# A streaming encoder step on one core: projection fills ranked by stage, merge weights in the fills' buffers, smaller pieces in the delta rule

## The chip, the cores and the metric

The kernel runs on one core of a Trainium2 chip. The metric is the device time of one execution in microseconds (us); it is the median of several executions. All arithmetic is float32: each big product is made of three matmuls of rounded parts (high by high, low by high, high by low), so one column block of weights always comes as a high tile (`whi`) and a low tile (`wlo`) that ScalarE and VectorE split from the raw block (`raw`).

## What is computed

The reference, cut to the parts that the change touches. 1152 tokens (a prompt of 1024 and 8 samples of 16) go through one layer of width 1024.

```python
h = rmsnorm(x)
z = h @ W_in                      # fq fk fv ff | gqkv ga gb gg | gate_a gate_b
yA = fox(fq, fk, fv, logf) @ w_proj_fox       # 8 heads x 64, 256 cached keys per sample
q, k, v = silu(short_conv(gqkv))              # width 4; its last 3 inputs are an output
o = gated_delta_rule(q, k, v, g, beta)        # chunks of 64 tokens, one after the other
yB = (rmsnorm(o) * silu(gg)) @ w_proj_gdn
x += rmsnorm((sigmoid(gate_a) * yA + sigmoid(gate_b) * yB) @ w_out)
x += rmsnorm(relu(rmsnorm(x) @ w_up) ** 2 @ w_down)
```

## The kernel before

The tokens are kept transposed, in high and low parts (`hhi`, `hlo`), as 9 tiles of 128 and 3 chunks of 384. The stages, in us of the profiled execution: the norm and the first transposes up to 50; the delta rule (GDN) for its four head pairs, 50 to 700; attention (FoX) for its four head pairs, 700 to 982; the merge, 982 to 1110; the output projection to 1227; the MLP to the end.

Each engine runs its instructions in a fixed order. That order is made ahead of time by a list scheduler that goes by priorities: `tc.high_priority(n)` ranks what is under it n places ahead of where it is written, and a negative n ranks it behind.

**Fills.** 32 column blocks of W_in are not needed where they are computed: gg, fq, fk and fv of the four head pairs (16 blocks, the list `todo`), then the merge's gates (16 more). Each is three chunks of 24 matmuls of 384 columns into the PSUM bank `mf`. ScalarE copies a chunk into the buffer `gst` and sends it to DRAM (`gg_d`, `fr_d`, `gate_d`), from where it is read back. `fill()` writes all of them (but the first) ahead of the delta rule with the priority -LOW, LOW = 100000: behind everything else, so that they run where TensorE has nothing else ready. Their weights lie in the pool `wp` (tag "f": FRB = 2 raw buffers, FHB = 3 high and low ones); the delta rule's own columns of W_in (bank `mm`) take theirs from `ww` (tag "w": RAWB = 1 raw buffer, 2 high and low ones).

**Delta rule.** For a head pair p, `gdn_in` multiplies the q, k and v columns; `gdn_conv` applies the convolution and the silu and sends out the last three inputs of the prompt and of each sample: a transpose on TensorE and a copy out of PSUM for each of 12 blocks, `lr` being the tile that GpSimd fills and that both go through. `gdn_systems` scales q, k and v and makes the decays and the systems of all 24 chunk units; `gdn_inverse` inverts them; `gdn_b` runs the recurrence over the chunks, for each of which TensorE waits in turn for `R` (L620), for `vn` (L623) and for `S` (L629) of VectorE. The copy `xs<-S` (L618) stands between them on VectorE. The products of `gdn_systems` over all 1152 tokens are single instructions on VectorE or GpSimd: on VectorE qs (L489), kb (L492), the decay's mask (L497) and half of qa (L508); on GpSimd vs (L477), ks (L486), the decay (L496) and the other half of qa (L508).

**Attention.** `fox_past` first reorders the columns of the cached log forget values by head pair with two GpSimd copies (L935), then transposes them on TensorE (L937).

**Merge.** `load` brings 24 blocks of attention and delta rule outputs back from DRAM (`orw`) and splits them into `ohi` and `olo`. For each of 8 column blocks j, `weights` loads and splits w_proj_fox and w_proj_gdn into buffers of the pool `op` (3 raw, 4 high and low), and six groups of 12 matmuls follow. A product with the sigmoid of a gate (`ga`) goes to `mt`; the sum of two is split into `hhi` and `hlo`, over the columns that the fills have been reading till then. `wo_part` loads the output projection's weights (`wor`).

## Time and profile before

| | |
|---|---|
| median of 3 executions | 1946.63 us (1942.45 to 1948.23) |
| the profiled execution | 1936.76 us, its span 1935.1 us |
| mean granted TensorE clock | 0.989 |
| TensorE busy | 1863.4 us, 96% of the span, 11036 matmuls |
| VectorE, ScalarE, GpSimd busy | 66%, 52%, 12% |

The profile is of one execution. A stretch of it is read by its busy times; a wait of an engine is named by the instruction that released it. TensorE runs nearly all the time, so a microsecond counts where TensorE stands still or works at a lower clock. A matmul's row is longer than its share of the time, since the next one starts before it ends.

### The profile page before, as it was taken

The numbers are of one execution on the slowest core, as the hardware profiler recorded it, in microseconds if no ns is written. First come the engines' busy times: TensorE is split into PE (matmuls) and PEld (weight loads), VectorE is DVE, ScalarE is ACT, GpSimd is POOL, SyncE is SP. The second block draws the span as 40 slices with busy tenths as digits, with TensorE's granted clock in tenths as the row PEclk, the third lists the DMA queues.
The fourth block names the chain that finished last, engine by engine and source line by source line (L and its number), as shares of the span: only waits on it lengthen the run. The fifth ranks groups of instructions, "written<-read, shape, count | busy, mean of one in ns | idle before, by whom it ended". The sixth has DMA issues, their size and how long they took to land.

```text
span 1935.1 us, 31957 instructions
## 1 busy us (share of the span) xinstructions
PE 1863.4 (96%) x11036; PEld 1689.2 (87%) x11036; DVE 1274.6 (66%) x3013; ACT 1001.1 (52%) x2382; POOL 232.6 (12%) x356
## 2 busy tenths in 40 slices
PE   7989999899999989999999999999999999999998
PEld 6979989899889987787899988999999998888886
DVE  6356587667774466766654455887677764559697
ACT  6344375464564665655554353555554554445553
POOL 2131251422512120000002200000000000000000
PEclk9999999999999999999999999999999999999999
DMA  6142413423335264433364462234444468845474
GB/s 197 45 102 69 114 47 91 106 63 106 84 87 166 76 186 141 132 109 110 89 196 138 139 206 89 65 115 131 139 137 132 145 186 296 289 149 183 149 261 137
DMA packets 293069, 261.34 MB, mean 135 GB/s; under 512 B 68876, under 2 KB 247368, under 8 KB 292908
## 3 DMA queue, kind: packets, MB, share of 16 engines
q1 hardware_dynamic: 252864, 225.10, 39.3%
q10 hardware_dynamic: 40044, 34.21, 5.4%
q8 instruction: 87, 1.43, 0.3%
q14 instruction: 74, 0.61, 0.1%
HBM read 186.48 MB, written 72.75 MB: 134 GB/s over the span
## 4 chain that ended last, share of the span: by engine, by line
PE 80%; DVE 6%; DMA 5%; ACT 4%; issue 3%; POOL 2%; SPq 0%; DVEq 0%; ACTq 0%; POOLq 0%
PE mm L158 47%; PE mf L158 14%; PE pc L1019 2%; PE pa L158 1%; PE pc L158 1%; PE pd L158 1%; PE pe L158 1%; PE pb L158 1%; DVE xs L618 1%; PE mm L1048 1%; DMA gate_d<-gst 1%; DMA out_dram<-kst 1%; PE pb L1010 1%; PE pc L633 1%; PE pa L461 1%
## 5 line engine op out<-in xcount | busy, mean ns | idle before, releaser
L158 PE MATMUL mf<-hhi,wlo 128*128 128x384 f32 x744 | 262.1, 353 | 2.4 <-DVE wlo L335 2.4
L158 PE MATMUL mf<-hhi,whi 128*128 128x384 f32 x744 | 261.1, 351 | 1.8 <-ACT gst L219 1.8
L158 PE MATMUL mf<-hlo,whi 128*128 128x384 f32 x744 | 261.9, 352 | 0.0
L158 PE MATMUL mm<-th,wh 128*128 128x320 f32 (+1 forms) x896 | 177.2, 293 | 0.0
L158 PE MATMUL mm<-bh,al 128*128 128x512 f32 x436 | 169.7, 389 | 0.0
L158 PE MATMUL mm<-bl,ah 128*128 128x512 f32 x436 | 169.6, 389 | 0.0
L158 PE MATMUL mm<-bh,ah 128*128 128x512 f32 x436 | 169.6, 389 | 0.0
L334 ACT CAST ah<-ar 128x512 fp32r<-128x512 f32 x107 | 66.4, 622 | 152.9 <-PE mm L158 101.1
L158 PEld LDWEIGHTS mf<-hhi,wlo 128*128 128x128 f32 x744 | 141.7, 190 | 3.6 <-DVE wlo L335 3.3
L158 PEld LDWEIGHTS mf<-hhi,whi 128*128 128x128 f32 x744 | 141.8, 191 | 2.4 <-ACT gst L219 2.1
L158 PEld LDWEIGHTS mm<-th,wh 128*128 128x128 f32 x896 | 142.9, 187 | 0.0
L158 PEld LDWEIGHTS mf<-hlo,whi 128*128 128x128 f32 x744 | 141.9, 191 | 0.7
L158 PE MATMUL mm<-th,wl 128*128 128x256 f32 x448 | 131.4, 293 | 0.0
L1381 DVE TENSOR_TENSOR s<-mm,s 128x256 f32<-128x256 f32 (+1 forms) x196 | 84.2, 453 | 66.2 <-PE mm L158 53.2
L335 DVE TENSOR_TENSOR al<-ar,ah 128x512 fp32r<-128x512 f32 x107 | 73.5, 688 | 74.6 <-ACT ah L334 73.9
L335 DVE TENSOR_TENSOR wlo<-raw,whi 128x512 fp32r<-128x512 f32 x110 | 76.8, 703 | 67.3 <-ACT whi L334 63.2
L158 PE MATMUL mm<-hhi,whi 128*128 128x384 f32 x288 | 103.9, 361 | 2.4 <-ACT whi L334 2.1
L158 PE MATMUL mm<-hhi,wlo 128*128 128x384 f32 x288 | 101.0, 351 | 2.1 <-DVE wlo L335 2.1
L158 PE MATMUL mm<-hlo,whi 128*128 128x384 f32 x288 | 102.5, 356 | 0.0
L334 ACT CAST whi<-raw 128x512 fp32r<-128x512 f32 x110 | 67.6, 620 | 62.2 <-PE mf L158 26.2
L158 PE MATMUL mm<-mhi,wl 128*128 128x256 f32 (+1 forms) x336 | 98.6, 293 | 0.0
L158 PE MATMUL mm<-mlo,wh 128*128 128x256 f32 (+1 forms) x336 | 98.6, 293 | 0.0
(543 smaller groups left out, 4949.3 us busy)
## 6 DMA issues: line engine op xcount, KB each, us to landing
ar<-ua_d SPq DMA_DIRECT2D x124, 256.0 KB
raw<-in_w_in_dram SPq DMA_DIRECT2D x86, 256.0 KB
br<-in_w_down_dram SPq DMA_DIRECT2D x78, 256.0 KB
wr<-in_w_up_dram SPq DMA_DIRECT2D x56, 256.0 KB
ua_d<-s SPq DMA_DIRECT2D x112, 128.0 KB
ua_d<-s ACTq DMA_DIRECT2D x84, 128.0 KB
gate_d<-gst ACTq DMA_DIRECT2D x48, 192.0 KB
ga<-gate_d SPq DMA_DIRECT2D x48, 192.0 KB
```

Of the source, the lines that this page charges most:

```text
L158: T.matmul(out, a, b, start=first and i == 0, stop=last and i == n - 1)
L334: A.copy(h, raw)
L335: V.tensor_tensor(l, raw, f(h), ALU.subtract)
L461: T.matmul(nps[:, t:t + NTT + 1:NTT], sq[:, t * P:(t + 1) * P], ones2, start=True, stop=True)
L618: (A.copy if h else V.tensor_copy)(xs[0:64, h], st_[64 * h:64 * h + 64])
L633: T.matmul(po[:, i * P:(i + 1) * P], xs[k0:].rearrange("p h c -> p (h c)"), qa[k0:, u].rearrange("p h c -> p (h c)"), start=True, stop=True)
L1010: T.transpose(tp[:, jj * 256 + qi * P:jj * 256 + qi * P + P], pr[qi][:, j * P:(j + 1) * P], ident)
L1019: T.matmul(acc[:, q0:256], v2[:, 2 * jp + jj, P * hh:P * hh + P], q[:, jj * 256 + q0:jj * 256 + 256], start=jp == 0 and jj == 0 and k == 0 ...
L1048: T.matmul(a[32 * b:32 * b + 32, P:384], qbd[:, b].rearrange("p h t -> p (h t)"), kt, start=True, stop=True)
L1381: V.tensor_tensor(r, o, x, ALU.add)
```

## The change

Seven edits: (1) `fill()` ranks the 15 first blocks 1400 places behind where they are written (RANKA) and the 16 gate blocks 3300 (RANKB), in place of 100000 for all; (2) more buffers: raw tiles of "w" 1 to 2, its high and low tiles 2 to 3, those of "f" 3 to 4, `gst` 1 to 2; (3) the last inputs of the convolution are kept in one tile `lrs` and go out once, at p == 2, by a function of their own, with 4 transposes a bank; (4) the convolution's prompt columns are done in two halves, after the samples; (5) the products qs, kb, the mask's sum and qa of the delta rule are done in halves; (6) the reordering of past's columns moves from the start of attention to p == 2 of the delta rule, into a tile of its own; (7) the merge's first weights (j == 0) take the fills' buffers, the others 2 raw and 3 high and low buffers in place of 3 and 4. Lines of the changed file lie up to 20 further down.

```diff
-RAWB = 1
+RAWB = 2
-FHB = 3
+FHB = 4
+RANKA = 1400
+RANKB = 3300
...
-    WBUFS = {"w": (RAWB, 2), "f": (FRB, FHB)}
+    WBUFS = {"w": (RAWB, 3), "f": (FRB, FHB)}
...
-               lambda c, acc: spill_out(wps_[tag], tag + "g", 1, w0, dst, c, acc), tag=(acc, nb), prio=prio)
+               lambda c, acc: spill_out(wps_[tag], tag + "g", 2, w0, dst, c, acc), tag=(acc, nb), prio=prio)
     def fill():
-        with tc.high_priority(-LOW):
-            for w0, dst in todo[NE:]:
-                spill(w0, dst, "f", "mf", 20, MFB)
+        for rank, part in ((RANKA, todo[NE:4 * NP_]), (RANKB, todo[4 * NP_:])):
+            with tc.high_priority(-rank):
+                for w0, dst in part:
+                    spill(w0, dst, "f", "mf", 20, MFB)
...
     def gdn_conv(gp, p, i, x):
-        lr = big(gp, "lr", 1, [P, 2, P])
-        G.memset(lr[:, 0], 0.0)
-        G.tensor_copy(lr[:, 0, 0:3], x[:, NPR:NPR + 3])
-        G.tensor_copy(lr[:, 0, 3:27].rearrange("p (b t) -> p b t", b=NB),
+        G.tensor_copy(lrs[:, 4 * i + p, 0:3], x[:, NPR:NPR + 3])
+        G.tensor_copy(lrs[:, 4 * i + p, 3:27].rearrange("p (b t) -> p b t", b=NB),
                       x[:, 3 + NPR:].rearrange("p (b t) -> p b t", b=NB)[:, :, 16:19])
-        lps = pt("pa", PAB)
-        T.transpose(lps[:, 0:P], lr[:, 0], ident)
-        A.copy(lr[:, 1], lps[:, 0:P])
-        cs = slice(512 * i + p * P, 512 * i + (p + 1) * P)
-        S.dma_start(conv_p[0, 0][:, cs], lr[0:3, 1])
-        S.dma_start(conv_s[0].rearrange("b t c -> (b t) c")[:, cs], lr[3:27, 1])
...
-        V.tensor_tensor(qs, qs, rq, ALU.mult)
+        for c in HALF:
+            V.tensor_tensor(qs[:, c], qs[:, c], rq[:, c], ALU.mult)
...
-            (G if h else V).tensor_tensor(qa[0:64, :, h], u3(qs)[hs], u3(gcb)[hs], ALU.mult)
+            for u in (slice(0, NU // 2), slice(NU // 2, NU)):
+                (G if h else V).tensor_tensor(qa[0:64, u, h], u3(qs)[hs, u], u3(gcb)[hs, u], ALU.mult)
...
+    def conv_out(gp):
+        for i in range(3):
+            lps = pt("pa", PAB)
+            for j in range(4):
+                T.transpose(lps[:27, j * P:(j + 1) * P], lrs[:, 4 * i + j], ident)
+            lr = big(gp, "be", BEB, [P, 512])
+            A.copy(lr[:27], lps[:27])
+            cs = slice(512 * i, 512 * (i + 1))
+            S.dma_start(conv_p[0, 0][:, cs], lr[0:3])
+            S.dma_start(conv_s[0].rearrange("b t c -> (b t) c")[:, cs], lr[3:27])
...
+            if p == 2:
+                conv_out(gp)
...
+            if p == 2:
+                for k in range(2):
+                    G.tensor_copy(clq[:, 64 * k:64 * k + 64].rearrange("p (q b h) -> p q b h", q=NP_, b=NB),
+                                  cl[:, k].rearrange("p (b q h) -> p q b h", b=NB, q=NP_))
...
     def fox_past(fp):
-        for k in range(2):
-            G.tensor_copy(cq[:, 64 * k:64 * k + 64].rearrange("p (q b h) -> p q b h", q=NP_, b=NB),
-                          cl[:, k].rearrange("p (b q h) -> p q b h", b=NB, q=NP_))
-        T.transpose(ct[:, 0:P], cq, ident)
+        T.transpose(ct[:, 0:P], clq, ident)
...
-        WBUFS["w"] = (3, 4)
+        WBUFS["w"] = (2, 3)
...
-            whi, wlo = weights([w_pf[0][:, js], w_pg[0][:, js]], "w", 200)
+            whi, wlo = weights([w_pf[0][:, js], w_pg[0][:, js]], "w" if j else "f", 200)
```

The order of the instructions changes most at three places. The first is ScalarE's order around the first column of the delta rule. A row is one instruction, what it writes, what it reads; `gst<-mf` copies a fill's chunk, `X<-mm` a chunk of the delta rule's columns, `whi<-raw` casts weights. Before:

```order
L219 COPY gst_374<-mf_349 128x384
L220 DMA gg_d<-gst_374 128x384
L219 COPY gst_502<-mf_477 128x384
L220 DMA gg_d<-gst_502 128x384
L395 COPY X_3587<-mm_3602 128x384
L774 ACT_TABLE_LOAD
L774 ACTIVATE qa_591<-qa_591 128x8
L395 COPY X_3587<-mm_3628 128x384
```

And with the change:

```order
L222 DMA fr_d<-gst_705 128x384
L221 COPY gst_745<-mf_720 128x384
L222 DMA fr_d<-gst_745 128x384
L221 COPY gst_773<-mf_748 128x384
L222 DMA fr_d<-gst_773 128x384
L336 CAST whi_902<-raw_900 128x512
L336 CAST whi_908<-raw_906 128x512
L221 COPY gst_801<-mf_776 128x384
L221 COPY gst_502<-mf_477 128x384
L222 DMA fr_d<-gst_801 128x384
L222 DMA gg_d<-gst_502 128x384
L399 COPY X_3589<-mm_3604 128x384
```

Before, three chunks of fills are copied ahead of the delta rule's first chunk; with the change nine are, and the weights of two more blocks are cast there. On TensorE 23.4 of the 96 chunks of fills now stand ahead of the first head pair's inversion (18.1 before), 64.2 ahead of the fourth's (56.5), 77.9 ahead of the first attention scores (70.0). Each tile of the delta rule's weights is now split 18 or more TensorE instructions ahead of its first use (5 to 18 before).

The second place is TensorE's order from attention to the merge. `pc<-phi,v` and `pc<-plo,v` are the last products of attention, `mf` is a fill, `pb<-ohi,whi` the first of the merge. Before:

```order
L158 MATMUL mf_3434<-hhi,wlo_3397 128x384
L1019 MATMUL pc_11138<-plo_11183,v_1931_10254 128x256
L158 MATMUL mf_3434<-hhi,whi_3402 128x384
L1019 MATMUL pc_11138<-phi_11182,v_1931_10254 128x128
L158 MATMUL mf_3434<-hlo,whi_3402 128x384
L1019 MATMUL pc_11138<-plo_11183,v_1931_10254 128x128
L158 MATMUL mf_3434<-hhi,wlo_3403 128x384
L158 MATMUL mf_3434<-hhi,whi_3402 128x384
```

And with the change:

```order
L1039 MATMUL pc_11150<-phi_11182,v_1912_10266 128x256
L1039 MATMUL pc_11150<-plo_11183,v_1912_10266 128x256
L1039 MATMUL pc_11150<-phi_11194,v_1912_10266 128x256
L1039 MATMUL pc_11150<-plo_11195,v_1912_10266 128x256
L1039 MATMUL pc_11150<-phi_11194,v_1912_10266 128x128
L1039 MATMUL pc_11150<-plo_11195,v_1912_10266 128x128
L160 MATMUL pb_11337<-ohi,whi_11329 128x384
L160 MATMUL pb_11337<-olo,whi_11329 128x384
```

Before, fills stand between the last products of attention, 80 more stand between these and the merge, and 26 in the merge itself; with the change the last fill ends at the last head pair's first cached keys (942.5 us in the trace of before), and the merge follows attention at once. From the middle of the merge on, the order of every engine is the same as before.

The third place is the queue of SyncE there. `fox_d<-oT` stores the last attention output, `orw` loads merge inputs, `wor` the output projection's weights. Before:

```order
L1075 DMA fox_d<-so_11063 128x64
L1091 DMA fox_d<-oT_10456 64x1024
L1151 DMA orw_11213<-gdn_d 128x384
L343 DMA raw_11309<-in_w_proj_fox_dram 128x4x128
L1171 DMA ga_11322<-gate_d 128x384
```

And with the change:

```order
L1095 DMA fox_d<-so_11075 128x64
L1158 DMA wor_11839<-in_w_out_dram 128x512
L1158 DMA wor_11843<-in_w_out_dram 128x512
L1111 DMA fox_d<-oT_10468 64x1024
L1158 DMA wor_11847<-in_w_out_dram 128x512
L1158 DMA wor_11851<-in_w_out_dram 128x512
L1171 DMA orw_11225<-gdn_d 128x384
L1191 DMA ga_11334<-gate_d 128x384
```

Two loads of `wor` now stand ahead of the store and two behind it, the latter into buffers that the former two must leave first; the first merge weights are no longer in this place, they are loaded earlier.

## Rows read from the trace of the kernel before

**Rows 1.** Page, parts 1 and 4: busy time by engine; chain by engine.

```profile
PE 1863.4 (96%) x11036; PEld 1689.2 (87%) x11036; DVE 1274.6 (66%) x3013; ACT 1001.1 (52%) x2382; POOL 232.6 (12%) x356
...
PE 80%; DVE 6%; DMA 5%; ACT 4%; issue 3%; POOL 2%; SPq 0%; DVEq 0%; ACTq 0%; POOLq 0%
```

**Rows 2.** Stretches: PE, PEld, DVE, ACT, POOL busy (count), clock, DMA share, GB/s.

```profile
50.00:700.00 650.00, 617.63 (x3722) 574.65 (x3721) 400.49 (x1113) 337.08 (x942) 187.82 (x272) 0.98 0.34 93
...
1227.00:1935.00 708.00, 700.95 (x4130) 640.18 (x4128) 516.36 (x1012) 350.42 (x761) 0.00 (x0) 1.00 0.54 170
```

**Rows 3.** What TensorE waited for: us in total, times, longest.

```profile
PE pb L621 <- DVE R L620: 7.1, 5, 2.0
...
PE pe L158 <- DVE mt L1176: 4.1, 1, 4.1
PE pb L626 <- DVE vn L623: 3.4, 2, 1.7
PE pa L438 <- POOL lr L435: 3.2, 7, 1.1
...
PE mf L158 <- DVE wlo L335: 2.4, 2, 1.7
PE mm L158 <- ACT whi L334: 2.1, 1, 2.1
PE mm L158 <- DVE wlo L335: 2.1, 1, 2.1
...
PE mf L158 <- ACT gst L219: 1.8, 2, 0.9
...
PE mm L937 <- POOL past L935: 1.6, 1, 1.6
```

**Rows 4.** Stretches after two long waits, and one in between; columns as before.

```profile
141.00:148.00 7.00, 6.12 (x22) 6.02 (x23) 3.50 (x11) 2.78 (x11) 1.28 (x3) 0.52 0.60 156
148.00:155.00 7.00, 6.95 (x44) 6.21 (x44) 3.97 (x13) 2.86 (x10) 2.75 (x5) 1.00 0.36 101
1045.00:1049.50 4.50, 3.22 (x11) 3.25 (x12) 4.17 (x9) 2.34 (x5) 1.97 (x2) 0.62 0.57 179
```

**Rows 5.** VectorE in time (start, duration, line): copies of the recurrence.

```profile
236.83 2.12 DVE L618 COPY xs<-S 64x64 f32<-64x64 f32 x1
...
249.49 0.18 DVE L618 COPY xs<-S 64x64 f32<-64x64 f32 x1
...
511.53 2.61 DVE L618 COPY xs<-S 64x64 f32<-64x64 f32 x1
```

**Rows 6.** GpSimd in time, at the two long copies.

```profile
236.26 2.64 POOL L486 TENSOR_TENSOR ks<-ks,y 128x1152 f32<-128x1152 f32 x1
...
511.38 2.71 POOL L508 TENSOR_TENSOR qa<-qs,gcb 64x1152 f32<-64x1152 f32 x1 [1.39 <-DVE qs L489]
```

**Rows 7.** The end of attention: all of it.

```profile
942.50:981.90 39.40, 38.95 (x255) 32.09 (x254) 21.55 (x60) 17.92 (x42) 1.14 (x4) 1.00 0.23 66
```

**Rows 8.** The fills' instructions alone, to the first merge matmul.

```profile
942.50:981.90 39.40, 21.32 (x89) 14.62 (x90) 0.00 (x0) 1.94 (x4) 1.00 0.23 66
981.90:995.90 14.00, 13.95 (x80) 13.63 (x79) 0.00 (x0) 1.44 (x3) 1.00 0.80 248
```

**Rows 9.** The chain of waits in time, at the end of attention.

```profile
962.69 3.88 DMA vc<-in_cache_fox_v_dram
...
971.19 1.91 PE mf L158 x11
```

**Rows 10.** SyncE's queue, first transfers after attention.

```profile
982.82 0.45 SPq L1091 DMA_DIRECT2D fox_d<-oT  x1
983.38 0.53 SPq L1151 DMA_DIRECT2D orw<-gdn_d  x1
```

**Rows 11.** ScalarE in time, the first cast of a merge input.

```profile
989.19 0.51 ACT L334 CAST ohi<-orw 128x384 fp32r<-128x384 f32 x1 [0.53 <-ACT gst L219]
```

**Rows 12.** TensorE, the first matmul of the merge.

```profile
995.90 0.44 PE L158 MATMUL pb<-ohi,whi 128*128 128x384 f32 x1
```

More of the change, by code (lines that the diff above doesn't have):

```diff
@@ L365, in tile_step @@
     cl = cb.tile([P, 2, 64], F32, name="cl")
+    clq = cb.tile([P, P], F32, name="clq")
     ngc = cb.tile([P, 1], F32, name="ngc")
@@ L422, in rows_bc @@
             S.dma_start(dst[64 * h:64 * h + 64], rows[h].partition_broadcast(64))
+    HALF = (slice(0, NT // 2), slice(NT // 2, NT))
     def u3(ap):
@@ L446, in gdn_conv @@
         av = a[:, NPR:].rearrange("p (b t) -> p b t", b=NB)
-        V.tensor_scalar(a[:, :NPR], x[:, 0:NPR], w[:, 0:1], None, ALU.mult)
         V.tensor_scalar(av, xv[:, :, 0:TS], w[:, 0:1], None, ALU.mult)
         for j in range(1, 4):
-            V.scalar_tensor_tensor(a[:, :NPR], x[:, j:j + NPR], w[:, j:j + 1], a[:, :NPR], ALU.mult, ALU.add)
             V.scalar_tensor_tensor(av, xv[:, :, j:j + TS], w[:, j:j + 1], av, ALU.mult, ALU.add)
+        for c0, c1 in ((0, 512), (512, NPR)):
+            V.tensor_scalar(a[:, c0:c1], x[:, c0:c1], w[:, 0:1], None, ALU.mult)
+            for j in range(1, 4):
+                V.scalar_tensor_tensor(a[:, c0:c1], x[:, j + c0:j + c1], w[:, j:j + 1], a[:, c0:c1], ALU.mult, ALU.add)
         A.activation(a, a, AF.Silu)
@@ L488, in gdn_systems @@
         rows_bc(rq, rows_n[0])
-        V.tensor_tensor(qs, qs, rq, ALU.mult)
+        for c in HALF:
+            V.tensor_tensor(qs[:, c], qs[:, c], rq[:, c], ALU.mult)
         kT = u3(ks)
         kb = ybig(gp)[:, :NT]
-        V.tensor_tensor(kb, ks, rb, ALU.mult)
+        for c in HALF:
+            V.tensor_tensor(kb[:, c], ks[:, c], rb[:, c], ALU.mult)
         dk = ybig(gp)[:, :NT]
@@ L496, in gdn_systems @@
         G.tensor_tensor(d3, u3(gcb), bc(cols[:, 0], 2, [P, NU, C]), ALU.subtract)
-        V.tensor_tensor(d3[:, :NUP], d3[:, :NUP], bc(madd, 1, [P, NUP, C]), ALU.add)
+        for u in (slice(0, NUP // 2), slice(NUP // 2, NUP)):
+            V.tensor_tensor(d3[:, u], d3[:, u], bc(madd, 1, [P, NUP // 2, C]), ALU.add)
         V.tensor_tensor(d3[:, NUP:], d3[:, NUP:], bc(madds, 1, [P, NU - NUP, C]), ALU.add)
@@ L896, in tile_step @@
         kds = [gp.tile([P, 2, P], F32, name=nm("kd")) for _ in range(2)]
+        lrs = gp.tile([P, 12, 27], F32, name="lrs")
         for kd in kds:
@@ L931, in fox_past @@
         ct = mmt()
-        cq = fp.tile([P, 4 * P], F32, tag="sp3", name=nm("past"))[:, :P]
-        for k in range(2):
-            G.tensor_copy(cq[:, 64 * k:64 * k + 64].rearrange("p (q b h) -> p q b h", q=NP_, b=NB),
-                          cl[:, k].rearrange("p (b q h) -> p q b h", b=NB, q=NP_))
-        T.transpose(ct[:, 0:P], cq, ident)
+        T.transpose(ct[:, 0:P], clq, ident)
         fl, on = (fp.tile([P, n * P], F32, tag=f"sp{n - 1}", name=nm("past"))[:64, :PAST + TS] for n in (6, 7))
```

## The prediction, made before the changed kernel was run

> **What bounds the kernel.** I read the page first, then the stretches by stage, then what TensorE waited for, and last the timeline of single places. The page shows TensorE busy for 96% of the span, VectorE for 66% [rows 1]: the time is TensorE's work plus what TensorE stands still or runs slow. The stretches show where: in the delta rule it is busy 617.6 of 650 us, in the MLP 701 of 708 at a full clock [rows 2]. In the waits the reader is to see that single waits of 1 to 4 us make up what can be won: the recurrence's R and vn, the merge's mt, the transposes of `lr`, weights (`whi`, `wlo`), `gst`, and past [rows 3]. The clock is the other part: behind the weight waits, from 141 us on, 7 us pass at a granted clock of 0.52, where TensorE does 22 matmuls; the next 7 us at 1.00 hold 44. Behind the mt wait 4.5 us have a mean of 0.62, which is 4.5 x 0.38 / 0.5 = 3.4 us at half and the rest full [rows 4]. 0.52 and 1.00 are its levels of 1.2 and 2.4 GHz. A matmul of 384 columns takes 1.91 / 11 = 0.174 us of TensorE's time at full clock [rows 9].
>
> The work on TensorE hardly changes (12 transposes stay 12). The fills' matmuls only change place, so moving them is worth the waits that it ends or opens, nothing more. The sum is made against the profiled execution, 1936.76 us; the median of the runs shown, 1946.63, lies 9.87 us (0.5%) higher, and I apply the difference to the median.
>
> **The change part by part: gains.**
>
> *Weights of the delta rule and the fills.* More buffers and the new ranks put each split 18 or more TensorE instructions ahead of its first use, where 5 was usual. 18 matmuls are 18 x 0.174 = 3.1 us, more than the longest of the weight waits, 2.1 [rows 3]. I count all three lines as gone: 2.4 + 2.1 + 2.1 = 6.6 us. They also end the stretch of half clock: 22 matmuls instead of 44 in 7 us is 3.5 us, of which a little is a wait; I take 3.4. Both could come back elsewhere, since the delta rule's first column now comes six chunks of fills later (6 x 24 x 0.174 = 25 us); that is a rival below.
>
> *The convolution's outputs.* 3.2 us of waits for `lr` in 7 places [rows 3] go; GpSimd's copies stay, but nothing waits for them until p == 2. The 12 transposes then stand together, 4 to a bank, with GpSimd long done. Gain 3.2. The 6 stores in place of 24 are off TensorE's path; they shorten SyncE's queue, which I cost at nothing.
>
> *`gst` in two buffers* ends the wait for the store of the buffer before: 1.8 [rows 3]. *Past's columns* are ready long before attention: 1.6 [rows 3]. GpSimd does the same two copies at p == 2, ahead of delta rule products of its own; by its 12% it has room [rows 1].
>
> *The halves.* R and vn cost 7.1 + 3.4 = 10.5 us [rows 3]. Their cause is seen in VectorE's copies xs: 0.18 us as a rule, but 2.12 at 236.83, ending as GpSimd's ks product from 236.26 does, and 2.61 at 511.53, ending with GpSimd's half of qa from 511.38 [rows 5, 6]. The change halves qa on GpSimd, not ks, vs or the decay. Halving lets a copy through some 2.7 / 2 = 1.35 us earlier; qa stands at one wait of 2.0 and both of vn, so 3 x 1.35 = 4 us at best there. The bounds are 0 (the second half holds the next copy instead) and 10.5 (every such wait ends); I take 2.0, half of the 4, since for each copy let through there is a second piece behind. *The trace thus shows long copies that end with GpSimd's instruction.* The Trainium skill ("SBUF — State Buffer", section "Who interferes with whom") says that VectorE's copy and GpSimd share ports under an exclusive lock that is held for the whole instruction; by it the three products that stay whole keep their waits, and the trace agrees in the two ends above. Its "Perfetto Trace Analysis" ("Optimizing Scalar/DVE Operations") says the other: breaking up instructions that cause bubbles may let work be done sooner; by that alone all R and vn waits could go, which is the first rival.
>
> *The merge.* mt waits 4.1 us because the merge's first sums are written over the columns that the last fills still read; these fills are gone from there. With it goes the half clock behind, 3.4 us at half speed: 1.7 [rows 3, 4]. The merge's weights in three buffers instead of four are cast one group of 12 matmuls ahead (12 x 0.174 = 2.1 us), which covers the cast and the difference; I cost them at nothing, and if the cover fails it is a fraction of a microsecond for each of 7 blocks.
>
> Together: 6.6 + 3.4 + 3.2 + 1.8 + 1.6 + 2.0 + 4.1 + 1.7 = 24.4 us.
>
> **Losses.** *The end of attention.* From 942.5 to 981.9 us TensorE was busy without a gap, 39.4 us, with 89 fills among its 255 matmuls [rows 7, 8]. The 89 are 89 x 0.174 = 15.5 us; the rest is 23.9. Without them the stretch ends somewhere between 23.9 us (no loss) and 39.4 (a loss of 15.5: VectorE's 21.6 us and ScalarE's 17.9 one after the other are 39.5, so the chain of score, softmax, transpose, split and product could need it all). Neither end is nearer: VectorE and ScalarE overlap in part. I take the middle, a loss of 7.8.
>
> *Ahead of the merge.* 80 fills, 14.0 us, filled the time from the last attention output to the first merge matmul at 995.9 [rows 8, 12]. Now TensorE stands still there: the store is issued at 982.82, the first `orw` load behind it at 983.38, the first cast of one was at 989.19 [rows 10, 11]. From 982.8 to that cast are 6.4 us, the cast is 0.5, its low part about as much, and a little for the half that waits for the store's reading back: 8.0. Bounds: 3.9, the time of one load (vc, twice as large) [rows 9], and the 14.0, since `wor` loads now stand in the queue behind and ahead of the store. After such a stop I expect the half clock as after mt: 1.7.
>
> Losses 7.8 + 8.0 + 1.7 = 17.5, net 24.4 - 17.5 = 6.9 us faster: 1946.63 - 6.9 = **1939.7 us**. About 0.3% (5.8 us) is what a measurement of this kernel can tell from no change, so this is a small but visible gain.
>
> **The rivals.**
>
> *The halves free the recurrence and the end of attention stays full.* VectorE gets R, vn and S between halves, so all 10.5 us of R and vn go instead of 2.0; attention's chain overlaps and needs only the 23.9 us of TensorE. For it: VectorE's halves stand between the recurrence's steps in the new order. Against it: ks, vs and the decay stay whole [rows 6]. It gives 8.5 + 7.8 more: 6.9 + 16.3 = 23.2 faster, 1923.4 us.
>
> *The cover is used up* (the slower side). Attention's end is bound by its chain and stays at 39.4 us; the loads ahead of the merge take 14.0; behind both the clock is at half, twice 1.7. Losses 15.5 + 14.0 + 3.4 = 32.9 against 24.4: 8.5 slower, 1955.1 us. For it: VectorE's and ScalarE's 39.5 us of work there [rows 7], and two more transfers ahead of the `orw` loads. Against it: each end of the two ranges must hold at once. It decides from losses of 30.2 on (24.4 + 5.8).
>
> *The weight waits only move.* The delta rule begins 25 us later with the same VectorE chain in it; what TensorE no longer waits for weights it waits for columns or the convolution. The 6.6 and the 3.4 stay: 6.9 - 10.0, so 3.1 slower, 1949.7 us. For it: the R and vn waits show that VectorE's chain, not the supply of weights, holds TensorE in several places [rows 3]. Against it: more fills stand between the delta rule's steps at first.
>
> That the change doesn't do what it says I leave out: the order of the instructions shows the fills moved.
>
> **The numbers.** Forecast 0.40, first rival 0.24, cover used up 0.20, waits only move 0.16. The forecast's own range goes from 14 faster to 1 slower, about 1932 to 1948; of its 0.40 I put 0.26 at more than 0.3% faster and 0.14 within. The last rival has 0.12 within 0.3% and 0.04 slower. Faster by over 0.3%: 0.24 + 0.26 = 0.50; within: 0.14 + 0.12 = 0.26; slower: 0.20 + 0.04 = 0.24. The range reaches to the first rival and to the second, with a few us for their own bounds: 1920 to 1956.
>
> **What would show it.** In the changed profile: no line of waits for `whi` or `wlo` over 1 us in the delta rule and no half clock near 140 to 170 us; no waits for `lr`, past or mt; waits for R and vn that remain beside vs, ks and the decay. The stretch from the last head pair's first cached keys to the end of attention should take 30 to 33 us with TensorE busy for some three quarters; TensorE should stand still some 8 us ahead of the merge. The prediction is wrong if that stretch takes under 26 or over 37 us, if the stop is under 4 or over 13, or if the delta rule up to the first attention scores, with its eight more chunks of fills (8 x 4.2 us), does not gain 10 us or more on its own work.

## The result, and the profile after

The changed kernel takes 1953.76 us (median of 6, 1950.12 to 1961.22), the kernel before 1945.87 in the same comparison: the ratio is 1.0063, with a 95% interval of 1.0042 to 1.0084. By the ratio it is some 12 us slower (0.63% of 1946), by the two medians 7.9; forecast were 6.9 us faster. The profiled execution took 1952.47 us with a span of 1950.8, 15.7 above the span before; the one before had been 9 us below its median, this one is 1.3 below, so the 15.7 overstates the difference by a few us.

On the page (busy times, and the granted clock in 40 slices) TensorE is busy for the same 96% [rows 1], with the same number of matmuls. One slice, 975 to 1024 us, where attention ends, has a clock of 0.7:

```profile
PE 1879.8 (96%) x11036; PEld 1697.6 (87%) x11036; DVE 1281.5 (66%) x3077; ACT 998.6 (51%) x2373; POOL 231.9 (12%) x348
...
PEclk9999999999999999999979999999999999999999
```

The list of what TensorE waited for (us in total, times, longest) answers to [rows 3]:

```profile
PE pb L160 <- ACT ohi L336: 8.5, 3, 7.5
...
PE pe L596 <- ACT kd L607: 5.7, 2, 5.2
...
PE pb L625 <- DVE R L624: 5.1, 4, 1.7
...
PE pd L625 <- DVE R L624: 2.9, 6, 0.8
...
PE pa L461 <- ACT y L459: 2.1, 1, 2.1
...
PE mm L160 <- ACT X L399: 1.6, 1, 1.6
...
PE pd L160 <- ACT whi L336: 1.1, 1, 1.1
...
PE pb L630 <- DVE vn L627: 0.9, 1, 0.9
```

The waits for `lr`, past and mt are gone, those for weights in the delta rule too, `vn` fell from 3.4 to 0.9 (2.3 in the second profile of the changed kernel, 1.7 in that of before). In their places stand a wait of 5.2 us for `kd`, one for the column squares (`y`), one for `X`, and 7.5 us for `ohi` ahead of the merge. R has 5.1 and 2.9.

The end of attention, from the last head pair's first cached keys to the last product, its last third alone, and the stop ahead of the merge (columns as in [rows 2]):

```profile
994.00:1007.80 13.80, 12.85 (x55) 9.89 (x53) 7.85 (x18) 5.61 (x12) 0.00 (x0) 0.60 0.13 40
...
966.30:1007.80 41.50, 33.86 (x169) 24.36 (x168) 20.08 (x57) 15.02 (x35) 1.12 (x4) 0.79 0.19 55
...
1007.80:1015.60 7.80, 0.32 (x2) 0.18 (x2) 3.10 (x6) 3.30 (x7) 0.00 (x0) 0.77 0.67 205
```

It takes 41.5 us with two matmuls of fills at its start and none after, more than the 39.4 with 89 of them [rows 7, 8]; the mean clock is 0.79, in the last third 0.60. The stop is 7.8 us. Between them these two explain a loss, but not what became of the 24 us of gains. The following places show that.

The first block's matmuls (weights `ew`; durations as min/median/max ns, then the start of the first and the last in us), before and with the change:

```profile
L158 PE MATMUL mf<-hhi,ew x48: 332/336/449, 18.8 to 51.7; 128*128 128x384 f32 x48
```

```profile
L160 PE MATMUL mf<-hhi,ew x48: 331/336/448, 18.8 to 78.1; 128*128 128x384 f32 x48
```

And ScalarE in time, where the delta rule's first column is copied out in the changed kernel:

```profile
78.62 0.85 ACT L221 COPY gst<-mf 128x384 f32<-128x384 f32 x2
80.05 0.48 ACT L399 COPY X<-mm 128x384 f32<-128x384 f32 x1 [0.58 <-ACT gst L221]
```

Before, the last `ew` matmul was at 51.7 us and the first copy of `X` at 52.9; now they are at 78.1 and 80.0. The delta rule starts 27 us later. The last products of attention (the same columns) show that this lateness is still there at the end:

```profile
L1019 PE MATMUL pc<-plo,v x160: 222/281/455, 705.5 to 981.7; 128*128 128x256 f32 x128, 128*128 128x128 f32 x32
```

```profile
L1039 PE MATMUL pc<-plo,v x160: 219/282/583, 743.1 to 1007.8; 128*128 128x256 f32 x128, 128*128 128x128 f32 x32
```

981.7 - 52.9 = 928.8 us from the first `X` to the last product before, 1007.8 - 80.0 = 927.8 now.

### The profile page after: what moved, and what is told of

Its sections match the earlier page's. It is cut to its first block, busy times and chain, and to the rows that moved or that the text cites. A ratio compares the mean times of both kernels' runs of the same rounds, so it can differ in the third digit from the quotient of the medians.

```text
span 1950.8 us, 32025 instructions
## 1 busy us (share of the span) xinstructions
PE 1879.8 (96%) x11036; PEld 1697.6 (87%) x11036; DVE 1281.5 (66%) x3077; ACT 998.6 (51%) x2373; POOL 231.9 (12%) x348
```

## The experiments

Where a text speaks of what TensorE loses in a stretch, it is the sum over its matmuls of the time from one start to the next beyond the usual one for that size (the length that a third of them fall below), so waits and half clock together. The first score is the first product of queries and keys in attention. All ratios are to the kernel before, run on the same chip.

**The ranks, or the rest?**

```diff
 no_ranks (the change with)
-RANKA = 1400
-RANKB = 3300
+RANKA = 100000
+RANKB = 100000
```

> The changed kernel with both groups of fills ranked last again (100000), all other edits kept. Theory A (the ranks cost the time: they leave the end of attention and the start of the merge without fills, where TensorE then waits and falls to half clock): the stretch from the last head pair's first cached keys to the last attention product takes 39 to 41 us again (41.5 in the changed kernel, but with 89 fills' matmuls back in it), the stop ahead of the merge is under 1.5 us, and the time is 12 to 25 us below the changed kernel, 1930 to 1942. Theory B (other edits cost it: merge weights in the fills' buffers, loads of the output weights ahead in the queue): the time stays within 5 us of the changed kernel, 1949 to 1959.

Ratio 0.9976 (0.9959 to 0.9994). The end of attention takes 36.9 us (943.5 to 980.4; 39 to 41 were expected), TensorE loses 2.8 there, and 0.2 up to the merge. Without its ranks the change is a small gain. The counterpart is the kernel before with the new `fill()` alone:

> The kernel before with the two ranks alone. By its order 93.8 of the 96 chunks of fills are done at the last head pair's first cached keys (96.0 in the changed kernel, 87.9 before). Theory A: the end of attention and the stop ahead of the merge lose 12 to 25 us together (3 before), nothing else gains more than 8: 1951 to 1966. Theory B: within 5 us of the kernel before, 1941 to 1951.

1.0074 (1.0053 to 1.0094). TensorE loses 9.7 at the end of attention and 14.0 ahead of the merge. So the ranks cost 0.7 to 0.9%, with or without the other edits. That was theory A's forecast for the time, but both kernels differ in more than the end, as was to be seen.

**The other edits, one at a time.** Four kernels were made of the one before.

```diff
 gst2_only
-lambda c, acc: spill_out(wps_[tag], tag + "g", 1, w0, dst, c, acc)
+lambda c, acc: spill_out(wps_[tag], tag + "g", 2, w0, dst, c, acc)
```

> The kernel before with the spill buffer gst doubled and nothing else. In attention up to the last head pair's cached keys TensorE lost 40.5 us before and 29.4 with the change. Theory C (a fill's copy on ScalarE waits for the store of the one before, and the copies kst behind it in ScalarE's queue wait too): the waits for gst and kst (1.8 and 6.1 us) go, that stretch loses 30 to 34 us, the time is 6 to 11 us below the kernel before. Theory D (the gain came from the order that the ranks make): that stretch loses 38 to 42 us and the time is within 3 us of before.

0.9960 (0.9944 to 0.9977): 7.7 us, as theory C has it for the time. Its list of waits shows only part of the reason; the line of before stands first:

```profile
PE pb L1010 <- ACT kst L883: 3.1, 3, 1.5
```

```profile
PE pb L868 <- ACT kst L871: 3.0, 3, 2.0
...
PE mf L158 <- ACT gst L219: 1.8, 2, 0.9
...
PE pb L1010 <- ACT kst L883: 0.4, 1, 0.4
```

The second `kst` line fell from 3.1 to 0.4, `gst` itself stayed at 1.8, and the stretch loses 36.4, between the two forecasts (40.5 and 44.4 in the two profiles of before). The profiled execution of this kernel was 7.7 above its median, so where the rest of the gain sits is open.

```diff
 bufs_only
-RAWB = 1
+RAWB = 2
-FHB = 3
+FHB = 4
-    WBUFS = {"w": (RAWB, 2), ...
+    WBUFS = {"w": (RAWB, 3), ...
-        WBUFS["w"] = (3, 4)
+        WBUFS["w"] = (2, 3)
-... "w", 200)
+... "w" if j else "f", 200)
```

> The kernel before with the buffers of weights alone (delta rule: 2 raw, 3 high and low; fills: 4; the merge's 2 and 3, its first weights in the fills' buffers), gst single. Theory E (weight waits in the delta rule stand in front of a wait for its VectorE and ScalarE chain of the first head pair, which takes their place): up to the first attention score TensorE loses 99 to 104 us (102.2 before, 103.0 changed) and the time is within 4 us of before. My prediction's step: that loss falls by 8 to 12 us and the time by as much.

1.0014 (1.0000 to 1.0027). No weight wait is left in the delta rule and nothing is won. Near 140 us, where before 2.1 and 2.1 us of weight waits stood on either side of 1.3 for `kqt`, one wait is left, as long as the three:

```profile
PE pa L520 <- ACT kqt L517: 5.9, 1, 5.9
```

The profiled execution, at the top of this kernel's runs, loses 120.8 up to the first score, more than either side expected; only that it didn't fall can be said.

The halves of qs, kb, the mask's sum and qa alone (the diff is that of the change):

> The kernel before with the halves of qs, kb, the mask's sum and qa and nothing else. My prediction's step: R and vn waits (10.5 us before) lose about 2, the time is 1 to 4 us lower. First rival of the prediction: they lose 8 or more, the time is 7 to 11 us lower. Theory G: the halves open as much as they close (each piece on GpSimd shuts out the next copy): within 2 us.

0.9999 (0.9988 to 1.0009). R has 8.4 us and `vn` 1.9:

```profile
PE pb L627 <- DVE R L626: 5.5, 5, 1.8
...
PE pd L627 <- DVE R L626: 2.9, 7, 0.7
...
PE pd L632 <- DVE vn L629: 1.4, 2, 1.1
...
PE pb L632 <- DVE vn L629: 0.5, 1, 0.5
```

Before, R had 7.1 on the line of [rows 3] and 1.6 under the other bank:

```profile
PE pd L621 <- DVE R L620: 1.6, 4, 0.8
```

So R is as it was. `vn` had 3.4 before, but 1.7 in the second profile of before, so that it fell by the halves is not shown. And `kd` waits 4.8 where it had 0.2. The convolution's outputs at once, its halves, and past's columns (edits 3, 4 and 6):

> The kernel before with the convolution's outputs kept in one tile and sent out at once, the convolution's prompt columns in halves, and past's columns reordered in the delta rule; nothing else. My prediction's step: the waits for lr (3.2) and past (1.6) go and the time falls by 3 to 6 us. Theory E for these (the wait behind takes their place): no wait for lr or past in the list, and the time within 2 us of before.

1.0016 (1.0001 to 1.0031). `lr` and past are gone from the list, 4.8 us, but R has 14.5 in place of 8.7 and `kqt` 5.1 in place of 1.3:

```profile
PE pb L620 <- DVE R L619: 7.4, 7, 1.6
...
PE pd L620 <- DVE R L619: 7.1, 6, 2.0
...
PE pa L519 <- ACT kqt L516: 5.1, 2, 3.6
```

These parts together, without ranks and weight buffers:

> The changed kernel without the ranks and without the added weight buffers and the merge's weights in the fills' buffers: left are gst doubled, the convolution's outputs, the halves, past. If the parts add up (gst alone 0.4% below before, the buffers alone 0.1% above, all three kinds together 0.24% below), it is 0.3 to 0.7% below the kernel before. If the buffers are what lets the others gain, it is within 0.2% of it.

0.9957 (0.9944 to 0.9970), within the noise what the doubled `gst` gives alone.

**Is it the end of attention?** If missing cover costs the time, putting it back must win it back. Some fills were held by a copy of one element over their raw tile, which has to wait for a tile of attention.

```diff
 held4 (the change with)
-... (RANKB, todo[4 * NP_:])):
+... (RANKB, todo[4 * NP_:-4])):
+                if touch:
+                    G.tensor_copy(raw[0:1, 0, 0:1], touch[0])
                 S.dma_start(raw, ...)
...
+                    if p == 3 and not hh and s == 0:
+                        touch.append(late[5][0:1, 0:1])
+                        with tc.high_priority(-LOW):
+                            for w0, dst in todo[-4:]:
+                                spill(w0, dst, "f", "mf", 20, MFB)
+                        touch.clear()
```

> The changed kernel, ranks and all, but the last four of the 16 gate blocks can load their weights only when the third head pair's attention output begins to be written (one element of it is copied over the raw tile first). By its order 90.0 of the 96 chunks are done at the last head pair's first cached keys, 93.3 at the last attention product, 95.0 at the first merge matmul (96.0 three times in the changed kernel). Theory A (missing fills at the end of attention and ahead of the merge cost the time): that stretch takes 38 to 42 us with 3.3 chunks in it and loses 2 to 5 us (20 in the changed kernel), the stop ahead of the merge is under 2 us (7.5), and the time is 15 to 25 us below the changed kernel, 0.2 to 0.8% below the kernel before. Theory F (the ranks cost by what they move to the front, not by what they take from the end): the time is within 5 us of the changed kernel, 0.4 to 0.8% above the kernel before.

1.0062 (1.0048 to 1.0076): nothing won, theory F's number. The end of attention is repaired, 37.3 us at full clock:

```profile
965.50:1002.80 37.30, 36.72 (x247) 30.80 (x245) 21.84 (x59) 17.84 (x41) 1.13 (x4) 1.00 0.22 70
```

But the stock of fills is out earlier, and for 38 us there is none (the fills' instructions alone); from the first score to the last head pair's first cached keys TensorE loses 50.9 us, 29.4 in the changed kernel:

```profile
831.00:869.00 38.00, 0.00 (x0) 0.00 (x0) 0.00 (x0) 0.00 (x0) 0.91 0.44 132
```

So I let the last eight blocks go in steps (the same edit with four release points), so that fills are spread as before:

> The changed kernel, ranks and all, with the last eight of the 16 gate blocks let go in steps along attention: two when the first head pair's output begins to be written, two with the second's, one with the third's, three in the middle of the third's. By its order the chunks of fills done are 72.0 at the first attention score (77.9 changed, 70.0 before), 75.5, 77.6, 81.3, 83.2 and 86.9 along attention, 88.5 at the last head pair's first cached keys, 92.3 at the last product, 94.0 at the first merge matmul: as the kernel before within 1.5 throughout. Theory H (fills are a stock of cover; the ranks spend 8 chunks of it ahead of attention, where little is won by it, and a hole of that size opens wherever the stock is out): no stretch of attention loses over 12 us more than before, the end of attention loses 2 to 5, the stop ahead of the merge under 1.5, and the time is 10 to 22 us below the changed kernel, 0.1 to 0.6% below the kernel before. Theory F (the ranks cost by what they move into the delta rule): within 5 us of the changed kernel.

1.0101 (1.0081 to 1.0122), the slowest of all. Theory H fell: the cover was as before along attention, within 1.5 chunks, and the time was not. TensorE waited 18 us at the start of attention:

```profile
PE pa L1008 <- POOL smask L972: 18.0, 1, 18.0
```

GpSimd in time shows what it waited for, the last head pair's outputs of the delta rule, each behind a DMA; first in this kernel, then in the changed one:

```profile
721.11 0.99 POOL L661 TENSOR_TENSOR be<-be,be 128x384 f32<-128x384 f32 x1 [15.53 <-DMA be<-rows_o]
...
729.91 0.99 POOL L661 TENSOR_TENSOR be<-be,be 128x384 f32<-128x384 f32 x1 [3.40 <-DMA be<-rows_o]
...
733.13 0.25 POOL L972 MEMSET smask<- 128x192 f32 x1
```

```profile
721.13 1.02 POOL L657 TENSOR_TENSOR be<-be,be 128x384 f32<-128x384 f32 x1 [4.34 <-DMA be<-rows_o]
...
726.28 1.01 POOL L657 TENSOR_TENSOR be<-be,be 128x384 f32<-128x384 f32 x1 [4.14 <-DMA be<-rows_o]
...
729.52 0.25 POOL L968 MEMSET smask<- 128x192 f32 x1
```

Both reach the same place within 4 us, with 72 chunks of fills done here and 78 there. From the first `X` to the first score it takes 653.4 us here, with 62.8 chunks in between, and 649.8 in the changed kernel, with 68.7. No copy that holds a fill has run yet (the first is at 746.3 us). 25 us less work for TensorE did not bring attention forward. Behind that point the copies stand in GpSimd's queue, so a part of what held4 and spread lose in attention may be theirs; that was not tried apart.

**Useless work at the end.**

```diff
 dummy4 (the change with; the last lines at the end of fill())
+NDUM = 4
...
+        last_w[:] = weights(halves(win, w0), tag, prio)
...
+        with tc.high_priority(-LOW):
+            hi, lo = last_w
+            for r in range(NDUM):
+                acc = pt("mf", MFB)[:, :CH]
+                mm3(acc, [pr for k in range(KT) for pr in (
...
```

> The changed kernel with four more chunks of 24 fill matmuls whose result nobody reads (96 matmuls, 16.7 us of useless work at full clock), ranked last; by the order 3.2 of them fall between the last attention products and 0.8 ahead of the merge. Theory I (a good part of what the end of attention loses is the clock, which falls to half where TensorE has little to do): that stretch takes at most the 41.5 us of the changed kernel although it holds 77 more matmuls, its granted clock is 0.95 or more (0.79 in the changed kernel), and the time is 2 to 10 us below the changed kernel. Theory J (the chain of ScalarE and VectorE sets that stretch, the clock only follows): the stretch and the time are within 2 us of the changed kernel, or up to 6 above.

The stretch is shorter with 77 more matmuls, at a clock of 1.00:

```profile
964.90:1002.60 37.70, 37.20 (x246) 30.75 (x246) 19.99 (x57) 14.97 (x35) 1.12 (x4) 1.00 0.17 47
```

37.7 us against 41.5, and 40.9 in a second profile of the changed kernel. For the stretch theory I is right. The time is 1.0069 (1.0046 to 1.0092), that of the changed kernel in the same comparison 1.0071, so a gain of 3 to 4 us in the time is not shown; for the time theory J's number came in.

Second profiles, of both kernels:

> The changed kernel once more, on the chip of these comparisons: 0.5 to 0.9% above the kernel before; a second profile, whose losses by stretch differ from the first by how much such numbers vary between executions: I expect under 3 us at the end of attention and ahead of the merge and up to 6 us in the delta rule.

> The kernel before once more, for a second profile. The first was of an execution some 9 us below the median. I expect the difference in the delta rule: up to the first attention score TensorE loses 105 to 112 us here (102.2 in the first), the end of attention and the stop ahead of the merge 2 to 5 as in the first.

1.0071 (1.0052 to 1.0090) for the changed kernel. Up to the first score TensorE lost 107.3 (103.0 in the first profile), at the end of attention and ahead of the merge 26.8 (27.8). Before: 102.5 up to the first score (102.2), so I was wrong there; the 4 us more lay in attention. Differences of 4 to 6 us between two profiles mean nothing in the delta rule or along attention; at the end of attention two profiles of one kernel lie within 0.6 us.

**What the ranks delay.** `early_mm`, the first block, is ranked -LOW on its own line, and the change leaves that: all other fills now pass it. The delta rule's first tiles are in pools that are opened after the first stage's pool, which holds `ew`, is closed. GpSimd's first write of such a tile (`tt`) waited for a matmul of `mf`, before and with the change:

```profile
52.06 0.57 POOL L559 MEMSET tt<- 32x576 f32 x1 [34.60 <-PE mf L158]
```

```profile
74.00 0.57 POOL L563 MEMSET tt<- 32x576 f32 x1 [45.60 <-PE mf L160]
```

TensorE had the first column's first chunk ready long before (the changed kernel; the other two thirds of the chunk end with it):

```profile
L160 PE MATMUL mm<-hhi,wlo x8: 333/338/339, 23.2 to 27.7; 128*128 128x384 f32 x8
```

It stood in PSUM for 52 us. In ScalarE's order its copy `X` stands behind the first block's last copy, and in each kernel with that block it starts 1.2 to 3.1 us after the last `ew` matmul began. That `X` too waits there for the first stage's memory, and not for something else of that block, is read from the code and not shown.

```diff
 early1000 (the change with, in early_mm)
-            with tc.high_priority(-LOW):
+            with tc.high_priority(-1000):
```

> The changed kernel, both ranks of the fills kept, with one number more changed: the first block (early_mm), which stays ranked last (100000) in the change while all other fills move ahead of it, is ranked 1000. The delta rule's first tiles lie where that block's weights (ew) lay, so they wait for its last matmul: at 51.7 us before, 78.1 in the changed kernel. Theory K (the ranks cost because the fills overtake this one block, and with it the whole chain delta rule, attention, merge starts some 27 us later; how TensorE is filled matters less): last ew matmul at 50 to 54 us, first attention score at 700 to 712 (730 to 734 changed), chunks of fills there 70.5 (77.9), and the time is 14 to 22 us below the changed kernel, 0.0 to 0.5% below the kernel before. Theory A alone (fills missing at the end of attention): the same order there, so it can't be told apart by the time, but by the start. Theory F (the ranks as such): within 5 us of the changed kernel.

0.9993 (0.9977 to 1.0010). The `ew` row:

```profile
L160 PE MATMUL mf<-hhi,ew x48: 332/336/522, 19.1 to 52.4; 128*128 128x384 f32 x48
```

One number brings the start of the delta rule back to 53.7 us, and with both ranks kept the loss is gone. This kernel has fills at the end of attention again, too (4.8 chunks are left there), so alone it can't tell the start from the end; held4 and spread, which start at 80 us and have fills at the end, still lose. Two trials of an earlier end of that block, on the kernel without ranks and buffers (`NE = 0`; `high_priority(-0)` in `early_mm`):

> The best kernel so far (gst doubled, convolution outputs, halves, past, without ranks and added weight buffers; 0.43% below the kernel before) without the early block: NE = 0, all 32 blocks are fills. Theory K: the delta rule's second chunk starts at 42 to 50 us in place of 55, and the time falls 3 to 10 us below that kernel, 0.6 to 0.9% below the kernel before. Against it: TensorE has less to do while the norms run, and what it loses there (under 10 us) eats the earlier start: within 3 us of that kernel.

> The best kernel so far with the early block ranked where it is written (0 in place of 100000): it ends some microseconds earlier by the order, ahead of the last casts of hhi. Theory K: last ew matmul 1 to 4 us earlier, the time 1 to 4 us below that kernel. Otherwise within 2 us of it.

ne0: 0.9937 (0.9915 to 0.9959). `X` starts at 32.6 us, 20 earlier, and the last attention product is at 967.7, 9 earlier than in its parent; the time is some 4 us below it (0.9957), the intervals meet. nb_early0: 0.9964 (0.9946 to 0.9982), no difference; its last `ew` matmul stayed at 51.6, where 1 to 4 us earlier was expected.

**The dose.** `fill()` written behind the first column, the first, second or third of its blocks held until that column has begun:

```diff
 front1 (the change with)
+                if touch:
+                    G.tensor_copy(raw[0:1, 0, 0:1], touch[0])
                 S.dma_start(raw, ...)
...
-    def fill():
+    def fill(t):
...
                 for w0, dst in part:
+                    n = todo.index((w0, dst)) - NE
+                    if n == 1:
+                        touch.append(t)
                     spill(w0, dst, "f", "mf", 20, MFB)
+                    touch.clear()
...
                    hhi, hlo, KT, ev)
+            if p == 0 and i == 0:
+                fill(x[0:1, 3:4])
...
-        fill()
```

> The changed kernel with ranks; fill() is written behind the delta rule's first column and its second block can load its weights only when that column has begun (one element copied), so that by the order 6 chunks of fills stand ahead of the first column (9 in the changed kernel, 3 before), 74.0 ahead of the first attention score (77.9, 70.0), 91.5 at the last cached keys (96.0, 87.9). Theory K: the start of the second chunk of the first column is half way, 66 to 72 us (55.4 before, 83.1 changed), and so is the time: 0.1 to 0.5% above the kernel before. Theory H (what counts is whether fills are left at the end of attention; 4.5 chunks are): the time is that of before or below.

0.9942 (0.9924 to 0.9961), the time that theory H has, though its account had fallen with spread. The start was as forecast (`X` at 65.8, the second chunk at 66.3), but the kernel gained, so theory K's price for a late start was wrong by itself. Its `ew` and last products:

```profile
L160 PE MATMUL mf<-hhi,ew x48: 331/336/522, 18.8 to 64.5; 128*128 128x384 f32 x48
```

```profile
L1048 PE MATMUL pc<-plo,v x160: 221/281/389, 723.5 to 984.3; 128*128 128x256 f32 x128, 128*128 128x128 f32 x32
```

The other two doses:

> As front1, but the first block of the fills is held, not the second: 3 chunks ahead of the delta rule's first column, as in the kernel before; 91.6 chunks done at the last attention product, 4.4 left behind it. Theory L (the delta rule and attention are one chain of some 918 to 929 us from the first X to the last attention product, whatever fills it holds; the time is the start of the chain, the chain, and behind it 935 us with no fill left or 927 plus 4.2 us for each chunk left): first X at 52 to 55 us, last product at 972 to 982, the profiled span 1920 to 1938, ratio 0.994 to 1.000. Against it (front1 gained by the hold itself): as front1, 0.992 to 0.996 with the chain under 915.

> As front1, but the third block is held: 9 chunks ahead of the first column as in the changed kernel, none left behind attention. Theory L: first X at 76 to 81 us, last product at 995 to 1009, nothing to win behind it: span 1933 to 1950, ratio 1.000 to 1.007; between front1 and this, 12 us of delay buy 1.4 chunks (6 us) less behind attention and open a stop of some 7 us ahead of the merge. Against it: ratio under 0.997.

front0: 0.9965 (0.9951 to 0.9980), front2: 1.0056 (1.0036 to 1.0076); theory L's ranges for the start, the last product, the span and the ratio held for both. Its 935 us behind the chain with no fill left, and 927 and 4.2 for each chunk, were 6 to 7 too few: 941.0 in front2, and 952.5 in front0 for 945.5. From the timelines (us; "left" are chunks of fills behind the last attention product):

| kernel | first X | last product | between | left | from there to the end |
|---|---|---|---|---|---|
| before | 52.9 | 981.7 | 928.8 | 4.4 | 953.4 |
| before, again | 52.8 | 983.4 | 930.6 | 4.4 | 955.9 |
| changed | 80.0 | 1007.8 | 927.8 | 0 | 943.0 |
| changed, again | 79.8 | 1011.5 | 931.7 | 0 | 943.5 |
| early1000 | 53.7 | 979.3 | 925.6 | 4.8 | 958.5 |
| front0 | 53.2 | 975.6 | 922.4 | 4.4 | 952.5 |
| front1 | 65.8 | 984.3 | 918.5 | 1.4 | 942.4 |
| front2 | 79.3 | 1005.8 | 926.5 | 0 | 941.0 |
| held4 | 79.8 | 1002.8 | 923.0 | 2.7 | 947.8 |
| spread | 80.0 | 1009.3 | 929.3 | 3.7 | 951.7 |
| dummy4 | 80.2 | 1002.6 | 922.4 | 0.8 useless | 942.7 |

The middle is 918 to 932 us in all eleven rows and 922 to 932 in the other kernels (but 937 in ranks_only; 935 in ne0, which starts amid the norms), though it holds 83 chunks of fills in spread and 90 in dummy4 (3 of them useless), a difference of some 29 us of TensorE's work. How it would be far from these numbers was not tried. The time is the start, this middle, and what is left behind it. Moving fills ahead of the delta rule costs their whole length there, and pays back only those that stood behind attention, 4.4 x 4.2 = 18 us, less the stop of 7.8 that opens when none is left (10.4 is measured). From front0 to front1, three chunks more cost 12.6 and take 10.1 off the end; front1's middle is also the shortest. The next three (front2) cost 13.5 and take off 1.4. Two profiles of one kernel differ in the middle by 1.8 (before) and 3.9 (changed), so the 3 us between early1000 and front0 mean nothing, and the 7 to front1 may be more; why front1 beats early1000 by half a per cent is shown only in part. front1 and ne0 are the fastest of all these kernels.

## Why the prediction was wrong

The step that failed stands ahead of the forecast's sum: "The fills' matmuls only change place, so moving them is worth the waits that it ends or opens, nothing more." It is right of TensorE's work and wrong of the time, since the delta rule and attention are a chain that does not get shorter with fewer fills in it. I had the number, "6 x 24 x 0.174 = 25 us" later for the first column, and priced it only in a rival, at 10 us of waits. Measured it is 27.1 us, of which 10.4 come back behind attention; with 1.0 from the middle that is the whole 15.7 between the two spans. That such parts add up is no proof; early1000, held4, spread and the three doses show which of them is the cause. I also saw in the order that the first block's copy had fallen back to the ninth place ahead of `X` (the row `gst_502` in the first place shown) and did not ask why the block was last, and who waits for its end.

In the terms of the forecast's sum the same two profiles read so, as what TensorE loses: 0.8 us more up to the first score, where gains of 16.8 were forecast (6.6, 3.4, 3.2, 1.6 and 2.0); 11.1 less from there to the last head pair's first cached keys (1.8 forecast, for `gst`); 17.1 more at the end of attention (7.8); 7.5 more ahead of the merge (8.0); nothing in the merge (4.1 less forecast). Of the signs of being wrong two came: the end of attention took over 37 us, and the delta rule gained nothing. The rival of used-up cover gave 1955.1, near the measured time; that is luck, for it has the gains of 24.4 in it, most of which did not come.

*Gains in the delta rule (6.6 + 3.4 + 3.2 + 2.0).* The waits for weights, `lr` and past went as I said, the time did not; R kept its waits. bufs_only, conv_past and halves_only, each the edit alone, are at 1.0014, 1.0016 and 0.9999. That is my third rival's mechanism, the waits only move; it gave 1949.7, since it had the other gains in it. One place shows it in the changed kernel, where the weights had been waited for: GpSimd's decay product ends at 153.9, ScalarE's exponential follows, and the copies from PSUM stand behind it in its queue; on VectorE a half of `qa` stands ahead of a part of `kd`.

```profile
151.81 2.12 POOL L498 TENSOR_TENSOR y<-gcb,cols 128x1152 f32<-128x1152 f32 x1
```

```profile
153.96 1.17 ACT L503 ACTIVATE gcb<-gcb 128x1152 f32<-128x1152 f32 x1 [3.22 <-POOL y L498]
...
155.15 0.20 ACT L603 COPY R<-pe 64x64 f32<-64x64 f32 x1
```

```profile
156.94 1.76 DVE L512 TENSOR_TENSOR qa<-qs,gcb 64x576 f32<-64x576 f32 x1
158.73 0.28 DVE L605 TENSOR_SCALAR kd<-pe,tm 64x64 f32<-64x64 f32 x1
```

```profile
160.06 0.47 PE L596 MATMUL pe<-ident,ks 128*128 128x128 f32 x1 [5.24 <-ACT kd L607]
```

The wait for `kd`, 5.2 us, is as long as what it replaces: 2.1 + 2.1 for weights [rows 3] and 1.3 for another tile between them. In the same place bufs_only waits 5.9 for `kqt`, and halves_only, without a buffer more, 3.8 for `kd` and not for weights. The half clock behind it is there again too (columns as in [rows 2]):

```profile
160.00:165.00 5.00, 4.94 (x19) 4.84 (x20) 1.96 (x5) 2.25 (x8) 1.01 (x3) 0.50 0.77 184
```

*Halves.* I took 2.0 of bounds of 0 to 10.5; measured is 0 (0.9999, 0.9988 to 1.0009). The Trainium skill's rule in "Perfetto Trace Analysis" ("Optimizing Scalar/DVE Operations"), that breaking up instructions may let work finish sooner, gave the first rival; no run here shows it for these products, halves_only decides against. The Trainium skill's rule in "SBUF — State Buffer" ("Who interferes with whom"), that whole instructions hold the shared ports, would leave R as it was, and with 8.4 against 8.7 the trace agrees.

*`gst`.* I had 1.8; alone it is worth 7.7, though not through the wait I named, which stayed at 1.8. This term was mis-sized, by a factor of four.

*Past and `lr`.* 1.6 and 3.2 were forecast; the edits alone cost 0.16%.

*The merge.* The mt wait of 4.1 went. The merge loses 9.4 us as before all the same: waits for `ohi` and its first weights, up to 1.1 us each, and behind the stop a half clock of 6.6 us (4.4 us at 0.50, then 5.0 at a mean of 0.78), where I had expected one of 3.4.

*The end of attention.* I took 31.7 us, the middle of 23.9 and 39.4. It took 41.5, beyond the bound, since I counted the clock only behind the stop: 0.79 on average. The work alone, with 77 useless matmuls for company, takes 37.7. That speaks for the chain of VectorE and ScalarE, as the slower rival had it; but TensorE's rows are busy for 37.2 of these 37.7 us, so the chain's own length is not shown.

*Ahead of the merge.* 8.0 forecast, 7.8 measured.

Right were, then, which waits would end and the price of the stop, and in part the slower rival's picture of attention's end. But that rival could not have been made into the result by its own means: held4 mends that end and wins nothing, though it opens a hole earlier.

## What to carry to other kernels

Before fill work is moved, ask which chain the time follows, and whether what is moved starts that chain later: here a few chunks of fills more or less did not change the length of such a chain, and cost their full length ahead of it. When ranks are changed, look for the one piece of work that keeps its old rank, and for who waits for its end. A list of single waits is not a sum of gains; undo or do one part alone before adding them up.

## What the runs showed of the hardware that I had not expected

In the last 13.8 us of attention without fills TensorE was granted 0.60 on average, between its levels of 1.2 and 2.4 GHz, although its rows show it busy for 12.85 of them; in the 11.5 us before the clock fell they had been busy for 9.0. Work that nobody reads, 77 matmuls in the stretch, kept the clock at 1.00 and made the stretch 3 to 4 us shorter.
